# Expert stages of a two-block kernel: the steps of neighbouring expert pairs interleaved, with TensorE's order stated

## The chip, the cores and the metric

The kernel runs on one core of a Trainium2 chip. The metric is the device time of one execution in microseconds. The engines of a core run their own instruction queues in order: TensorE (PE; its weight loads are listed apart as PEld), VectorE (DVE), ScalarE (ACT), GpSimd (POOL) and SyncE (SP), which here issues the loads from HBM; they wait for each other through semaphores.

## The reference, cut to what matters

The program is two transformer blocks on 256 tokens of width 1024. The change concerns the hierarchical mixture of experts, which the second block computes twice, once in each of its two layers:

```python
def hier_moe(h, router_g, router_e, w1, w3, w2):
...
    pg = jax.nn.softmax(hf @ router_g.astype(f32), axis=-1)
    gi = jnp.argmax(pg, axis=-1).astype(jnp.int32)
...
    pk, ik = lax.top_k(jax.nn.softmax(le_sel, axis=-1), TOP_K)
    wts = pg_sel * pk / jnp.sum(pk, axis=-1, keepdims=True)
...
        return (jax.nn.silu(xi @ w1[e]) * (xi @ w3[e])) @ w2[e]
```

For each token a router picks one of four groups of eight experts and two experts in it; the two results are added with the router's weights. All 32 experts' w1, w3 (1024 x 512 each) and w2 (512 x 1024) are read in float32: six tiles of 1024 KB an expert, 192 a layer.

## The kernel before, in words

The function `moe` (line 1738) handles one layer. It gives each expert 64 places for tokens and takes the experts in 16 pairs; in a pair the two experts' tokens stand in the two halves of 128 columns, so that the matmuls of the two run side by side in TensorE's column halves (`tile_position`). The steps of a pair, in the generator `experts`, are:

- *gather* (line 1828): the tokens of four experts are selected by matmuls with 0/1 matrices, scaled (lines 1830 and 1831) and put into a buffer `xq`; half of a buffer with every pair, ahead of the two pairs that use it.
- *up* (line 1849): w1 and w3, two halves of the inner dimension, 32 matmuls of 64 columns by 512, into two PSUM banks `acc`.
- *pick* (lines 1856 to 1864): the selection matrix turned round, and the weights of the tokens.
- *hidden* (lines 1866 to 1868): tanh on ACT, two operations on VectorE, into a tile of the kind t2.
- *turn* (line 1872): four transposes into a bank `fb`, copied by ACT (line 1874) into another t2 tile.
- *down* (line 1884): w2, two halves c of the output, 16 matmuls into two `acc` banks.
- *evacuation* (lines 1888 to 1891): for each c a product with the gate on VectorE, a rounded copy on ACT and the remainder on VectorE, both t2 tiles.
- *scatter* (line 1895): for each c four matmuls that bring the result back to token order in a bank `mm`, added to x on VectorE (line 1896).

There are four `acc`, two `mm` and two `fb` banks, and four t2 tiles (two t2a, two t2b, taken in turn).

The weights of a stage are 192 tiles, loaded on SP's queue in the order of a list (`ExpertWeights`, line 1540, the load at line 1569) into a ring of 16 slots: nine shared with the large activations (`wa`), five (`w`) and two (`ww`). The first ones are loaded before the stage begins. `next` hands out the tiles in the order of the list, and issues the loads that follow in the ring.

Where each instruction stands in its engine's queue is not written out: a scheduler sets it when the program is built, from the program order as priority, the dependences and its own timing of them. After pair 28 (`OVER_AT`, line 180; pairs are named by their first expert) all loads that are left are issued and a test follows whether any expert has more than 64 tokens (`overflow`, line 1898); the branch behind it ends a block of the program, across which no instruction is moved. The last pair, 30, stands behind it.

Of the kernel before, what the change touches and what calls it, by code (L numbers as in the profile page):

```python
# [11 lines left out]
F32 = mybir.dt.float32  # L12
# [4 lines left out]
OP = mybir.AluOpType  # L17
# [190 lines left out]
def tile_blocks(ctx: ExitStack, tc: tile.TileContext, A, out):  # L208
# [1331 lines left out]
    class ExpertWeights:  # L1540
# [197 lines left out]
    def moe(l, x, cols_, router, weights):  # L1738
# [93 lines left out]

        gate = []

        def experts(xt, sel, ws_, load, n, s0=0, first=False):

            m = 64 * n
            ph = [bank("acc"), bank("acc")]  # L1840
            for kq in range(2):
                if first:
                    gather(sel, xt, kq)
                for i, nm in enumerate(("w1", "w3")):
                    w = [load(nm, e, kq) for e in range(n)]
                    for k in range(4):
                        for e in range(n):
                            sl = slice(64 * e, 64 * e + 64)
                            PE.matmul(ph[i][sl], xt[:, 4 * kq + k, s0 + 64 * e:s0 + 64 * e + 64],  # L1849
                                      w[e][:, k * 512:(k + 1) * 512], start=kq == 0 and k == 0, stop=kq == 1 and k == 3,  # L1850
                                      tile_position=(0, 64 * e))

            ps = bank("fb")
            f32 = [z.bitcast(F32) for z in sel]
            for t in range(2):
                PE.transpose(ps[:m, t * P:(t + 1) * P], f32[t][:, s0:s0 + m], ident)
            for e in range(n):
                for t in range(2):
                    PE.matmul(ps[64 * e:64 * e + 64, 256:257], f32[t][:, s0 + 64 * e:s0 + 64 * e + 64], ws_[:, t, e:e + 1],
                              start=t == 0, stop=t == 1, tile_position=(0, 64 * e), skip_group_check=True)  # L1860
            selw = temp(F32R)
            V.tensor_copy(selw[:m], ps[:m, :T])
            wsl_ = sm.tile([P, 1], F32, name="m_wsl", bufs=2)
            V.tensor_scalar(wsl_[:m], ps[:m, 256:257], 0.5, None, op0=OP.mult)
            th = temp2()
            S.activation(th[:m], ph[0][:m], AF.Tanh, scale=0.5)
            V.scalar_tensor_tensor(th[:m], th[:m], 1.0, ph[0][:m], op0=OP.add, op1=OP.mult)
            V.scalar_tensor_tensor(th[:m], th[:m], wsl_[:m], ph[1][:m], op0=OP.mult, op1=OP.mult)
            yield
            pt = bank("fb").rearrange("p (f s) -> p f s", s=P)  # L1870
            for f in range(4):
                PE.transpose(pt[:, f, :m], th[:m, f * P:(f + 1) * P], ident[:m, :m])
            ht = temp2().rearrange("p (f s) -> p f s", s=P)
            S.activation(ht[:, :, :m], pt[:, :, :m], AF.Copy)  # L1874
            if not gate:
                gate.append(gate_row(cols_, 5))
            gb, = gate
            py = [bank("acc"), bank("acc")]
            for c in range(2):
                w = [load("w2", e, c) for e in range(n)]  # L1880
                for f in range(4):
                    for e in range(n):
                        sl = slice(64 * e, 64 * e + 64)
                        PE.matmul(py[c][sl], ht[:, f, sl], w[e][:, f * 512:(f + 1) * 512], start=f == 0, stop=f == 3,  # L1884
                                  tile_position=(0, 64 * e))
            for c in range(2):
                cs = slice(c * 512, (c + 1) * 512)
                V.tensor_tensor(py[c][:m], py[c][:m], gb[:m, cs], op=OP.mult)  # L1888
                yh_, yl_ = temp2(F32R), temp2(F32R)
                S.activation(yh_[:m], py[c][:m], AF.Copy)  # L1890
                V.tensor_tensor(yl_[:m], py[c][:m], yh_[:m], op=OP.subtract)
                for t in range(2):
                    pa = bank(PAB)
                    for q in (yh_, yl_):
                        PE.matmul(pa, selw[:m, t * P:(t + 1) * P], q[:m], start=q is yh_, stop=q is yl_)  # L1895
                    V.tensor_tensor(x[:, t, cs], x[:, t, cs], pa, op=OP.add)  # L1896

        def overflow():

# [20 lines left out]
            with tc.If(many > 0):  # L1920
                V.scalar_tensor_tensor(slot, fq, -64.0, pos, op0=OP.mult, op1=OP.add)
                V.tensor_tensor(nx, xi, nx, op=OP.subtract)
                for t in range(2):
                    V.tensor_tensor(xid[:, t], fq[:, t], nx, op=OP.add)
                V.scalar_tensor_tensor(xid, fq, 0.0, xid, op0=OP.is_gt, op1=OP.mult)
                V.tensor_scalar(xid, xid, -1.0, None, op0=OP.add)
                V.memset(jt, 0.0)
                with tc.For_i(0, many, 1):
                    mk = st([2, 32], "mk")
                    V.tensor_scalar(mk, xid, jt, None, op0=OP.is_equal)  # L1930
                    sj = st([2, 32], "sj")
# [23 lines left out]
                    run(experts(xt, sel, sc[:, :, 1:2], load_at, 1, 0, True))  # L1955
# [93 lines left out]
```

## Time and profile before

| | |
|---|---|
| median of 3 runs | 2146.66 us (2145.38 to 2148.9) |
| the profiled execution | 2142.09 us, of which the span of its instructions is 2140.3 us |
| busy share of the span | PE 93%, PEld 59%, DVE 50%, ACT 29%, POOL 10% |
| HBM read | 585.95 MB, 276 GB/s over the span with what is written |
| weight tiles of the expert stages | 384 loads of 1024 KB (216 `wa`, 120 `w`, 48 `ww`) |
| up matmuls (line 1849) | 2048 records, about 600 ns each |

The two expert stages begin at 1022 and 1636 us, counted from the span's start. A busy time is the union of the records; TensorE's matmuls are pipelined and overlap, their ends are modelled, and each float32 matmul of 512 columns shows as two records. The idle time before an instruction is put down to the event that came last.

### The profile page before, as it was taken

The numbers are of one execution on the slowest core, as the hardware profiler recorded it, in microseconds if no ns is written. First come the engines' busy times: TensorE is split into PE (matmuls) and PEld (weight loads), VectorE is DVE, ScalarE is ACT, GpSimd is POOL, SyncE is SP. The second block draws the span as 40 slices with busy tenths as digits, with TensorE's granted clock in tenths as the row PEclk, the third lists the DMA queues.
The fourth block names the chain that finished last, engine by engine and source line by source line (L and its number), as shares of the span: only waits on it lengthen the run. The fifth ranks groups of instructions, "written<-read, shape, count | busy, mean of one in ns | idle before, by whom it ended". The sixth has DMA issues, their size and how long they took to land. (4 is left out here: it accounts for less than half of the span.)

```text
span 2140.3 us, 30475 instructions
## 1 busy us (share of the span) xinstructions
PE 1980.2 (93%) x12212; PEld 1256.9 (59%) x12212; DVE 1060.3 (50%) x2258; ACT 623.2 (29%) x1200; POOL 216.9 (10%) x419
## 2 busy tenths in 40 slices
PE   6999998999999899997999999998898999999896
PEld 5777787888988677776434333333795333333332
DVE  6787467866976477456323322222664233223223
ACT  4324655455555332433111111010442011111101
POOL 6475001110000160000000000000000000000000
PEclk8999999999999899999999999999998999999998
DMA  6532365545565236648799999997745999999992
GB/s 263 197 119 102 136 216 190 197 148 198 180 199 209 100 138 217 213 159 337 302 419 420 420 419 411 420 411 285 303 178 210 411 419 420 420 375 421 420 384 85
DMA packets 103650, 592.18 MB, mean 277 GB/s; under 512 B 30288, under 2 KB 30800, under 8 KB 32848
## 3 DMA queue, kind: packets, MB, share of 16 engines
q1 hardware_dynamic: 103360, 589.65, 70.3%
q8 instruction: 98, 1.61, 0.3%
q10 hardware_dynamic: 144, 0.52, 0.1%
q14 instruction: 48, 0.39, 0.1%
HBM read 585.95 MB, written 4.19 MB: 276 GB/s over the span
## 5 line engine op out<-in xcount | busy, mean ns | idle before, releaser
L1849 PE MATMUL acc<-wa,xq 128*64 128x512 f32 x1152 | 313.4, 602 | 2.5 <-DVEq L1920 2.5
L327 DVE TENSOR_TENSOR whl<-w,whl 128x1024 fp32r<-128x1024 f32 x203 | 255.2, 1258 | 111.7 <-ACT whl L325 109.9
L325 ACT ACTIVATE whl<-w 128x1024 fp32r<-128x1024 f32 x204 | 214.7, 1054 | 154.4 <-PE acc L405 71.0
L332 PE MATMUL mm<-hh,whl 128*128 128x256 f32 x736 | 215.1, 292 | 12.0 <-DVE hl L560 5.5
L334 PE MATMUL mm<-hh,whl 128*128 128x256 f32 x736 | 215.0, 292 | 2.0 <-DVE whl L327 1.9
L333 PE MATMUL mm<-hl,whl 128*128 128x256 f32 x736 | 212.3, 288 | 0.0
L1849 PEld LDWEIGHTS acc<-wa,xq 128*64 128x64 f32 x1152 | 93.1, 138 | 166.2 <-issue 157.5
L1849 PE MATMUL acc<-w,xq 128*64 128x512 f32 x640 | 183.0, 597 | 0.0
L332 PEld LDWEIGHTS mm<-hh,whl 128*128 128x128 f32 x736 | 145.2, 197 | 18.2 <-DVE hl L560 6.2
L334 PEld LDWEIGHTS mm<-hh,whl 128*128 128x128 f32 x736 | 144.9, 197 | 9.0 <-issue 4.0
L333 PEld LDWEIGHTS mm<-hl,whl 128*128 128x128 f32 x736 | 145.3, 197 | 1.3 <-issue 0.8
L1896 DVE TENSOR_TENSOR x<-x,mm 128x512 f32<-128x512 f32 x128 | 82.3, 684 | 93.9 <-PE mm L1895 93.9
L1888 DVE TENSOR_TENSOR acc<-acc,gb 128x512 f32<-128x512 f32 x64 | 44.8, 700 | 165.6 <-PE acc L1884 150.5
L1849 PEld LDWEIGHTS acc<-w,xq 128*64 128x64 f32 x640 | 54.3, 137 | 87.3 <-issue 83.5
L1830 DVE TENSOR_SCALAR xq<-mm,scnorm_ffn,ada_c 128x256 f32<-128x256 f32 x64 | 34.4, 543 | 128.2 <-PE mm L1828 67.5
L353 PE MATMUL mm<-hf,w 128*128 128x256 f32 x352 | 82.8, 384 | 1.9 <-DVE sz L1680 1.9
L1831 ACT ACTIVATE xq<-mm,ada_c,scnorm_ffn 128x256 f32<-128x256 f32 x64 | 35.6, 563 | 164.7 <-DVE xq L1830 164.7
L1884 PE MATMUL acc<-wa,t2b 128*64 128x512 f32 x288 | 74.5, 597 | 2.3 <-ACT t2b L1874 1.2
L1884 PE MATMUL acc<-wa,t2a 128*64 128x512 f32 x288 | 72.4, 596 | 2.3 <-ACT t2a L1874 1.2
L353 PEld LDWEIGHTS mm<-hf,w 128*128 128x128 f32 x352 | 64.5, 190 | 14.9 <-issue 2.4
L332 PE MATMUL acc<-hh,whl 128*128 128x256 f32 x224 | 66.0, 295 | 6.3 <-DVE x L583 5.6
L334 PE MATMUL acc<-hh,whl 128*128 128x256 f32 x224 | 65.2, 291 | 0.4 <-DVE whl L327 0.2
(812 smaller groups left out, 3765.5 us busy)
## 6 DMA issues: line engine op xcount, KB each, us to landing
wa<-in_w_dram SPq DMA_DIRECT2D x216, 1024.0 KB, 12.0
w<-in_w_dram SPq DMA_DIRECT2D x120, 1024.0 KB, 11.4
w<-in_ada_w_dram SPq DMA_DIRECT2D x48, 1024.0 KB, 4.9
ww<-in_w_dram SPq DMA_DIRECT2D x48, 1024.0 KB, 11.8
w<-in_w_up_dram SPq DMA_DIRECT2D x22, 1024.0 KB, 4.8
w<-in_wa_kv_dram SPq DMA_DIRECT2D x16, 1024.0 KB, 4.8
w<-in_wb_in_dram SPq DMA_DIRECT2D x12, 1024.0 KB, 4.8
w<-in_w_down_dram SPq DMA_DIRECT2D x11, 1024.0 KB, 4.8
```

The lines of the kernel that those rows point to most:

```text
L325: S.activation(h3, src, AF.Copy)
L327: (G if share and nsplit[0] % share == 0 else V).tensor_tensor(l3, src, h3, op=OP.subtract)
L332: PE.matmul(ps, ah, bh, start=start, stop=False)
L333: PE.matmul(ps, ah, bl, start=False, stop=False)
L334: PE.matmul(ps, al, bh, start=False, stop=stop)
L353: PE.matmul(ps, w3[:, k, j * P:(j + 1) * P], h[:, k], start=k == 0, stop=k == kt - 1)
L1830: V.tensor_scalar(xt[:, k0], ps[:, 0], a[:, k0:k0 + 1], b[:, k0:k0 + 1], op0=OP.mult, op1=OP.add)
L1831: S.activation(xt[:, k0 + 1], ps[:, 1], AF.Identity, scale=a[:, k0 + 1:k0 + 2], bias=b[:, k0 + 1:k0 + 2])
L1849: PE.matmul(ph[i][sl], xt[:, 4 * kq + k, s0 + 64 * e:s0 + 64 * e + 64], w[e][:, k * 512:(k + 1) * 512], start=kq == 0 and k == 0, stop=kq ...
L1884: PE.matmul(py[c][sl], ht[:, f, sl], w[e][:, f * 512:(f + 1) * 512], start=f == 0, stop=f == 3, tile_position=(0, 64 * e))
L1888: V.tensor_tensor(py[c][:m], py[c][:m], gb[:m, cs], op=OP.mult)
L1896: V.tensor_tensor(x[:, t, cs], x[:, t, cs], pa, op=OP.add)
```

## The change

The generator becomes a class with one method for each step, and the loop over pairs calls the steps of three pairs in turn: the turn of the pair before; the first half of up of this pair; the second scatter of the pair before last (`late`); the second half of up; pick and hidden; the gather; both halves of down of the pair before; its first scatter. `tc.issue_after(ins)` gives every instruction in its block that runs on the engine of `ins` (here TensorE) an edge of order behind `ins`, without a wait for its end. Before the overflow test and at the end of the stage a pair is finished by `rest`, without a neighbour. The list of loads is put in the same order: the w2 tiles of a pair behind the w1 and w3 tiles of the next.

```diff
@@ class ExpertWeights: the order of the loads @@
-            self.todo = [(nm, (l * 32 + e + j) * 2 + i) for e in range(0, 32, 2)
-                         for i, nm in ((0, "w1"), (0, "w3"), (1, "w1"), (1, "w3"), (0, "w2"), (1, "w2"))
-                         for j in range(2)]
+            ups, downs = ((0, "w1"), (0, "w3"), (1, "w1"), (1, "w3")), ((0, "w2"), (1, "w2"))
+            order, before = [], None
+            for e in range(0, 32, 2):
+                order += [(e, w) for w in ups] + [(before, w) for w in downs if before is not None]
+                before = e
+                if e == OVER_AT:
+                    order += [(e, w) for w in downs]
+                    before = None
+            order += [(before, w) for w in downs]
+            self.todo = [(nm, (l * 32 + e + j) * 2 + i) for e, (i, nm) in order for j in range(2)]
...
@@ the steps: a generator becomes a class with a method for each step @@
-        def experts(xt, sel, ws_, load, n, s0=0, first=False):
+        class Experts:
...
+            def up(self, kq):
...
+                return nc.cur_bb.bb.instructions[-1]
...
+            def turned(self):
...
+            def down(self, c):
...
+                py = bank("acc")
+                w = [self.load("w2", e, c) for e in range(self.n)]
...
+                last = nc.cur_bb.bb.instructions[-1]
+                V.tensor_tensor(py[:m], py[:m], gb[:m, c * 512:(c + 1) * 512], op=OP.mult)
                 yh_, yl_ = temp2(F32R), temp2(F32R)
-                S.activation(yh_[:m], py[c][:m], AF.Copy)
-                V.tensor_tensor(yl_[:m], py[c][:m], yh_[:m], op=OP.subtract)
+                S.activation(yh_[:m], py[:m], AF.Copy)
+                V.tensor_tensor(yl_[:m], py[:m], yh_[:m], op=OP.subtract)
+                self.y[c] = yh_, yl_
+                return last
...
+            def scatter(self, c):
...
+            def rest(self, late=None):
+
+                if late:
+                    late.scatter(1)
+                self.turned()
+                self.down(0)
+                with tc.issue_after(self.down(1)):
+                    for c in range(2):
+                        self.scatter(c)
...
@@ the loop over pairs in moe @@
+        before = late = None
         for e in range(0, 32, 2):
-            now = experts(xt, sel, wtf[:, :, e:e + 2], load, 2, 64 * (e % 4), e == 0)
-            next(now)
-            if e % 4 == 0 and e < 28:
-                nxt, nsel = big("xq", (8, 256)), slots(pos[:, :, e + 4:e + 8], 4)
-            if e < 28:
-                gather(nsel, nxt, e % 4 // 2)
-            run(now)
-            if e % 4 == 2:
+            now = Experts(xt, sel, wtf[:, :, e:e + 2], load, 2, 64 * (e % 4))
+            if before:
+                with tc.issue_after(behind):
+                    before.turned()
+            if e == 0:
+                gather(sel, xt, 0)
+            behind = now.up(0)
+            if late:
+                with tc.issue_after(behind):
+                    late.scatter(1)
+            if e == 0:
+                gather(sel, xt, 1)
+            behind = now.up(1)
+            now.picked()
+            now.hidden()
+            with tc.issue_after(behind):
+                if e % 4 == 0 and e < 28:
+                    nxt, nsel = big("xq", (8, 256)), slots(pos[:, :, e + 4:e + 8], 4)
+                if e < 28:
+                    gather(nsel, nxt, e % 4 // 2)
+                if before:
+                    before.down(0)
+                    behind = before.down(1)
+            if before:
+                with tc.issue_after(behind):
+                    before.scatter(0)
+            before, late = now, before
+            if e % 4 == 2 and e < 28:
                 xt, sel = nxt, nsel
             if e == OVER_AT:
+                before.rest(late)
+                before = late = None
                 weights.fill(192)
                 overflow()
+        before.rest(late)
```


The arithmetic of the steps stays. What stands outside the two expert stages keeps its order on every engine.

TensorE's queue in the program before, in the first layer, from the end of the up matmuls of one pair (lines 1849 up, 1872 turn, 1856 and 1859 pick, 1884 down):

```order
L1849 MATMUL acc<-wa,xq 64x512 x24
L1872 MATMUL fb<-ident,t2b 128x128 x4
L1856 MATMUL fb<-ident,t1b 128x128
L1856 MATMUL fb<-ident,t1a 128x128
L1859 MATMUL fb<-m_wt,t1b 64x1
L1859 MATMUL fb<-m_wt,t1a 64x1
L1859 MATMUL fb<-m_wt,t1b 64x1
L1859 MATMUL fb<-m_wt,t1a 64x1
L1884 MATMUL acc<-wa,t2a 64x512
```

The turn stands right behind up, and down right behind the turn and the pick.

TensorE's queue in the program before, the same pair, from the end of the first half of down to its scatter matmuls (line 1895; 1849 is the next pair's up):

```order
L1884 MATMUL acc<-wa,t2a 64x512
L1884 MATMUL acc<-w,t2a 64x512 x2
L1895 MATMUL mm<-t2b,t1a 128x512 x2
L1895 MATMUL mm<-t2a,t1a 128x512 x2
L1884 MATMUL acc<-w,t2a 64x512 x7
L1895 MATMUL mm<-t2b,t1a 128x512 x2
L1895 MATMUL mm<-t2a,t1a 128x512 x2
L1849 MATMUL acc<-w,xq 64x512
```

The first scatter stands one matmul behind the first half of down, the second right behind the second half. The first splits a couple of down matmuls, as the count of 7 behind it shows.

TensorE's queue in the changed program, in the first layer, from the gather (1835) over both halves of down (1903) and the first scatter (1919) to the turn (1889):

```order
L1835 MATMUL mm<-t1a,xh 128x256
L1835 MATMUL mm<-t1a,xl 128x256
L1903 MATMUL acc<-w,t2a 64x512 x8
L1903 MATMUL acc<-ww,t2a 64x512 x8
L1919 MATMUL mm<-t2a,t1b 128x512
L1919 MATMUL mm<-t2b,t1b 128x512
L1919 MATMUL mm<-t2a,t1b 128x512
L1919 MATMUL mm<-t2b,t1b 128x512
L1889 MATMUL fb<-ident,t2b 128x128 x4
```

Both halves of down now stand behind a gather, the first scatter behind both of them, and the turn, which is the next pair's, behind that.

TensorE's queue in the changed program, going on from that turn (1867 and 1870 pick, 1858 up, 1919 the second scatter):

```order
L1889 MATMUL fb<-ident,t2b 128x128 x4
L1867 MATMUL fb<-ident,t1b 128x128
L1867 MATMUL fb<-ident,t1a 128x128
L1870 MATMUL fb<-m_wt,t1b 64x1
L1870 MATMUL fb<-m_wt,t1a 64x1
L1870 MATMUL fb<-m_wt,t1b 64x1
L1870 MATMUL fb<-m_wt,t1a 64x1
L1858 MATMUL acc<-wa,xq 64x512 x16
L1919 MATMUL mm<-t2a,t1b 128x512
L1919 MATMUL mm<-t2b,t1b 128x512
L1919 MATMUL mm<-t2a,t1b 128x512
L1919 MATMUL mm<-t2b,t1b 128x512
```

Behind the turn and a pick come 16 up matmuls, and only then the second scatter of the pair whose down stood above.

## Rows read from the trace of the kernel before

**Rows 1.** Windows, both stages (busy us by engine, PEclk, DMA, GB/s).

```profile
1022.00:1472.00 450.00, 427.18 (x2012) 167.30 (x2010) 129.58 (x230) 53.48 (x94) 0.00 (x0) 1.00 0.99 408
...
1473.00:1485.00 12.00, 11.25 (x58) 4.28 (x60) 1.08 (x3) 0.00 (x0) 0.00 (x0) 1.00 0.01 3
...
1636.00:2094.00 458.00, 430.69 (x2012) 167.80 (x2010) 129.22 (x230) 53.45 (x93) 0.00 (x0) 0.99 0.98 401
...
2094.00:2125.00 31.00, 27.55 (x118) 9.33 (x117) 6.37 (x11) 3.13 (x7) 0.00 (x0) 0.94 0.01 3
```

**Rows 2.** The page: GB/s of the DMA in 40 slices.

```profile
GB/s 263 197 119 102 136 216 190 197 148 198 180 199 209 100 138 217 213 159 337 302 419 420 420 419 411 420 411 285 303 178 210 411 419 420 420 375 421 420 384 85
```

**Rows 3.** Source view of line 1872 (ns min/median/max, first, last start).

```profile
L1872 PE MATMUL fb<-ident,t2b x64: 272/273/331, 1041.6 to 1490.6; 128*128 128x128 f32 x64
...
L1872 PE MATMUL fb<-ident,t2a x64: 272/273/330, 1655.7 to 2114.0; 128*128 128x128 f32 x64
```

**Rows 4.** Timeline: first up of each stage, VectorE behind the last w2.

```profile
1021.98 0.64 PE L1849 MATMUL acc<-wa,xq 128*64 128x512 f32 x2
...
1501.72 0.70 DVE L1888 TENSOR_TENSOR acc<-acc,gb 128x512 f32<-128x512 f32 x1 [2.53 <-PE acc L1884]
...
1636.03 0.64 PE L1849 MATMUL acc<-wa,xq 128*64 128x512 f32 x2
...
2125.16 0.70 DVE L1888 TENSOR_TENSOR acc<-acc,gb 128x512 f32<-128x512 f32 x1 [2.53 <-PE acc L1884]
```

**Rows 5.** Waits of TensorE, 14 pairs of each stage (us, times, longest).

```profile
PE fb L1872 <- DVE t2b L1868: 9.2, 11, 0.9
...
PE mm L1895 <- ACT t2b L1890: 8.6, 8, 1.4
...
PE mm L1895 <- ACT t2a L1890: 12.5, 12, 1.4
...
PE fb L1872 <- DVE t2a L1868: 9.2, 11, 0.9
```

**Rows 6.** Timeline of TensorE: a pair with waits (idle in brackets).

```profile
1399.90 0.66 PE L1872 MATMUL fb<-ident,t2b 128*128 128x128 f32 x4 [0.88 <-DVE t2b L1868]
...
1406.41 0.73 PE L1895 MATMUL mm<-t2b,t1a 128*128 128x512 f32 x2 [0.67 <-ACT t2b L1890]
...
1412.87 0.73 PE L1895 MATMUL mm<-t2b,t1a 128*128 128x512 f32 x2 [1.42 <-ACT t2b L1890]
```

**Rows 7.** Timeline of TensorE: a pair nearly without waits.

```profile
1099.84 0.60 PE L1872 MATMUL fb<-ident,t2b 128*128 128x128 f32 x4
...
1101.12 7.09 PE L1884 MATMUL acc<-wa,t2a 128*64 128x512 f32 x32
...
1112.23 1.07 PE L1849 MATMUL acc<-wa,xq 128*64 128x512 f32 x2
...
1113.23 0.73 PE L1895 MATMUL mm<-t2a,t1a 128*128 128x512 f32 x2
...
1128.47 0.60 PE L1872 MATMUL fb<-ident,t2b 128*128 128x128 f32 x4
```

**Rows 8.** Source view of line 1569: loads from 1028, then from 1642.

```profile
L1569 SPq DMA_DIRECT2D wa<-in_w_dram x98: 327/328/1363, 1028.4 to 1441.1; - x98
...
L1569 SPq DMA_DIRECT2D w<-in_w_dram x55: 327/328/1034, 1047.9 to 1454.7; - x55
...
L1569 SPq DMA_DIRECT2D ww<-in_w_dram x22: 327/328/384, 1060.2 to 1458.1; - x22
...
DMA to landing us min/median/max: 4.8/12.7/18.0
...
L1569 SPq DMA_DIRECT2D wa<-in_w_dram x98: 327/328/423, 1642.6 to 2062.9; - x98
```

**Rows 9.** Windows, two stretches of the second stage (columns as Rows 1).

```profile
1875.00:1900.00 25.00, 23.12 (x108) 9.25 (x110) 5.33 (x11) 2.73 (x5) 0.00 (x0) 0.93 1.01 415
...
2025.00:2050.00 25.00, 22.91 (x94) 9.00 (x93) 6.44 (x10) 2.47 (x5) 0.00 (x0) 0.93 0.85 343
```

More of the change, by code (lines that the diff above doesn't have):

```diff
@@ L1833, in moe, with __init__ @@
         gate = []
-        def experts(xt, sel, ws_, load, n, s0=0, first=False):
[L1839 to L1843, printed above, removed]
+        class Experts:
+            def __init__(self, xt, sel, ws_, load, n, s0=0):
+                self.xt, self.sel, self.ws_, self.load, self.n, self.s0, self.m = xt, sel, ws_, load, n, s0, 64 * n
+                self.ph = [bank("acc"), bank("acc")]
+                self.y = [None, None]
+            def up(self, kq):
@@ L1844, in experts @@
                 for i, nm in enumerate(("w1", "w3")):
-                    w = [load(nm, e, kq) for e in range(n)]
+                    w = [self.load(nm, e, kq) for e in range(self.n)]
                     for k in range(4):
[L1847 to L1857, printed above, removed]
-                for t in range(2):
-                    PE.matmul(ps[64 * e:64 * e + 64, 256:257], f32[t][:, s0 + 64 * e:s0 + 64 * e + 64], ws_[:, t, e:e + 1],
-                              start=t == 0, stop=t == 1, tile_position=(0, 64 * e), skip_group_check=True)
-            selw = temp(F32R)
@@ L1862, in experts @@
[L1862 to L1880, printed above, removed]
-                for f in range(4):
-                    for e in range(n):
+                        for e in range(self.n):
+                            sl, c = slice(64 * e, 64 * e + 64), self.s0 + 64 * e
+                            PE.matmul(self.ph[i][sl], self.xt[:, 4 * kq + k, c:c + 64], w[e][:, k * 512:(k + 1) * 512],
+                                      start=kq == 0 and k == 0, stop=kq == 1 and k == 3, tile_position=(0, 64 * e))
@@ new lines, in up, with picked @@
+                return nc.cur_bb.bb.instructions[-1]
+            def picked(self):
+                ps, m, s0 = bank("fb"), self.m, self.s0
+                f32 = [z.bitcast(F32) for z in self.sel]
+                for t in range(2):
+                    PE.transpose(ps[:m, t * P:(t + 1) * P], f32[t][:, s0:s0 + m], ident)
+                for e in range(self.n):
+                    for t in range(2):
+                        PE.matmul(ps[64 * e:64 * e + 64, 256:257], f32[t][:, s0 + 64 * e:s0 + 64 * e + 64],
+                                  self.ws_[:, t, e:e + 1], start=t == 0, stop=t == 1, tile_position=(0, 64 * e),
+                                  skip_group_check=True)
+                self.selw = temp(F32R)
+                V.tensor_copy(self.selw[:m], ps[:m, :T])
+                self.wsl = sm.tile([P, 1], F32, name="m_wsl", bufs=2)
+                V.tensor_scalar(self.wsl[:m], ps[:m, 256:257], 0.5, None, op0=OP.mult)
@@ new lines, in hidden @@
+            def hidden(self):
+                m, ph = self.m, self.ph
+                th = self.th = temp2()
+                S.activation(th[:m], ph[0][:m], AF.Tanh, scale=0.5)
+                V.scalar_tensor_tensor(th[:m], th[:m], 1.0, ph[0][:m], op0=OP.add, op1=OP.mult)
+                V.scalar_tensor_tensor(th[:m], th[:m], self.wsl[:m], ph[1][:m], op0=OP.mult, op1=OP.mult)
+            def turned(self):
+                m = self.m
+                pt = bank("fb").rearrange("p (f s) -> p f s", s=P)
+                for f in range(4):
+                    PE.transpose(pt[:, f, :m], self.th[:m, f * P:(f + 1) * P], ident[:m, :m])
+                self.ht = temp2().rearrange("p (f s) -> p f s", s=P)
+                S.activation(self.ht[:, :, :m], pt[:, :, :m], AF.Copy)
@@ L1883, in experts @@
+            def down(self, c):
+                if not gate:
+                    gate.append(gate_row(cols_, 5))
+                gb, m = gate[0], self.m
+                py = bank("acc")
+                w = [self.load("w2", e, c) for e in range(self.n)]
+                for f in range(4):
+                    for e in range(self.n):
                         sl = slice(64 * e, 64 * e + 64)
-                        PE.matmul(py[c][sl], ht[:, f, sl], w[e][:, f * 512:(f + 1) * 512], start=f == 0, stop=f == 3,
+                        PE.matmul(py[sl], self.ht[:, f, sl], w[e][:, f * 512:(f + 1) * 512], start=f == 0, stop=f == 3,
@@ L1885, in experts @@
                                   tile_position=(0, 64 * e))
-            for c in range(2):
-                cs = slice(c * 512, (c + 1) * 512)
-                V.tensor_tensor(py[c][:m], py[c][:m], gb[:m, cs], op=OP.mult)
+                last = nc.cur_bb.bb.instructions[-1]
+                V.tensor_tensor(py[:m], py[:m], gb[:m, c * 512:(c + 1) * 512], op=OP.mult)
                 yh_, yl_ = temp2(F32R), temp2(F32R)
-                S.activation(yh_[:m], py[c][:m], AF.Copy)
-                V.tensor_tensor(yl_[:m], py[c][:m], yh_[:m], op=OP.subtract)
+                S.activation(yh_[:m], py[:m], AF.Copy)
@@ L1892, in experts @@
+                V.tensor_tensor(yl_[:m], py[:m], yh_[:m], op=OP.subtract)
+                self.y[c] = yh_, yl_
+                return last
+            def scatter(self, c):
+                m, cs = self.m, slice(c * 512, (c + 1) * 512)
                 for t in range(2):
                     pa = bank(PAB)
-                    for q in (yh_, yl_):
-                        PE.matmul(pa, selw[:m, t * P:(t + 1) * P], q[:m], start=q is yh_, stop=q is yl_)
+                    for i, q in enumerate(self.y[c]):
+                        PE.matmul(pa, self.selw[:m, t * P:(t + 1) * P], q[:m], start=i == 0, stop=i == 1)
@@ L1953, in load_at @@
                         return over
-                    run(experts(xt, sel, sc[:, :, 1:2], load_at, 1, 0, True))
+                    one_ = Experts(xt, sel, sc[:, :, 1:2], load_at, 1)
+                    for kq in range(2):
+                        gather(sel, xt, kq)
+                        one_.up(kq)
+                    one_.picked()
+                    one_.hidden()
+                    one_.rest()
                     V.tensor_scalar(jt, jt, 1.0, None, op0=OP.add)
```

## The prediction

> **What bounds the kernel now.** I read the windows of the two expert stages first, then what TensorE waits for in them, then single pairs in its timeline, then the weight loads, and last the ends of both stages.
>
> The reader is to see that two things are full at once. While the stage runs, the DMA engines are busy 0.99 and 0.98 of the time and TensorE 0.95 and 0.94 [rows 1]. One pair of experts is 12 tiles of 1 MB; at the 420 GB/s of the full slices a tile takes 1.0486 / 0.420 = 2.50 us [rows 2], a pair 30.0 us. TensorE's period is (1490.6 − 1041.6) / 15 = 29.9 us in the first stage and (2114.0 − 1655.7) / 15 = 30.6 in the second [rows 3]. The loads run in a ring of 16 slots, and a slot is given back by TensorE, so either side can hold the other.
>
> Which one ends last is decided at the ends. From 1473 to 1485 and from 2094 to 2125 the DMA share is 0.01 while TensorE works on [rows 1]; the last w2 matmul is done at 1501.7 and 2125.2, where VectorE takes it over [rows 4]. So about 30 us of landed weights lie unused when the stream ends. TensorE is the later of the two, and what it waits for is worth time until that stock is gone.
>
> It never waits for a load in the stretch of 14 pairs. It waits for ACT before the scatter matmuls (8.6 and 12.5 us) and for VectorE before the turning transposes (9.2 and 9.2) [rows 5]. In one bad pair this is 0.88 before the transposes, 0.67 before the first scatter and 1.42 before the second [rows 6]: each time the next step of the same pair stands next in TensorE's queue while its input is still being evacuated. (The gap shown is less than the loss, since the ends of the matmuls before it are modelled.)
>
> **The change part by part.**
>
> *Order of TensorE's steps.* Nothing is added or taken away: 32 up, 16 down, 8 scatter, 16 gather and 4 turn matmuls in a pair, and six small ones (an up or down matmul shows as two records). Moved: the turn goes behind the down matmuls of the pair before; down goes one pair later, behind the next pair's up and gather; the first scatter stands behind both halves of down; the second stands behind 8 to 16 up matmuls. What each used to wait for now runs beside 7 us of down, 3.5 us of the other half of down, or 3.4 us or more of up. The chain that these must cover is an evacuation of some 2 us, so I cost the waits at nothing; if the cover is gone (last pair before the overflow test, and the last pair of a stage, where nothing is interleaved) they stay as they are today.
>
> *Lone matmuls.* Two experts' matmuls run side by side in the two column halves: 32 records take 7.09 us. Where a scatter splits such a couple, 2 records alone take 1113.23 − 1112.23 = 1.00 us [rows 7]. The pair from 1099.84 to 1128.47 has no wait over 0.2 us and takes 28.6 us [rows 7], with four lone matmuls, that is two steps of 0.86 us lost. In the new order most pairs have none. 28.6 − 1.7 + 0.2 for one more change of kind = **27.1 us a pair**, against 30.0 of the loads.
>
> *TensorE's bound then.* Today a stage is 1501.7 − 1022.0 = 479.7 us = 16 × 29.9 + 1.3. New: 16 × 27.1 + 1.3, and about 8 us for the uncovered chains of the last two pairs: 443 us, ending at 1465 and, from 1636.0, at 2079 [rows 4].
>
> *Loads.* The list gives w2 one pair later, so it stays the order in which TensorE frees and needs the tiles; the same 192 tiles, each released by the last matmul that reads its slot. SP's queue holds the loads alone in this stretch, so nothing else is held up. 98 + 55 + 22 = 175 loads are issued after the ring is first full, from 1028.4; the quickest takes 4.8 us to land, 2.3 more than its transfer [rows 8]. 1028.4 + 2.3 + 175 × 2.5 = 1468.2. Today it is 1472, so some 4 us are lost to late slots; I keep 2 of them: 1470. The last two tiles land together and 16 of the 32 down records follow, 3.5 us: **1473.5**. This is later than TensorE's 1465: the loads bound the stage, with a margin of 8.5 us or 0.5 us a pair. In the second stage the loads begin at 1642.6 [rows 8]: 1642.6 + 2.3 + 437.5 + 2 + 3.5 = **2087.9**.
>
> *New waits.* Four tiles of the kind t2 carry six values a pair, and the hidden activations now keep theirs until the turn. So VectorE's subtraction for the second half must wait for the turn; behind it in VectorE's queue stand the selection copy and the adds that free the scatter banks. The turn is the next thing after the first scatter, and the second scatter comes 8 or more up matmuls later, so I take 0. No row shows this wait; its bounds are 0 and the 1.42 us of today's longest [rows 6], below nothing not, since it takes no work away. The same for the four acc banks: two for up, two for down, each evacuated one step before its next use: 0.
>
> *Clock.* TensorE will now wait for loads in the last third of a stage. Waiting has cost clock here: two stretches of 25 us have a granted clock of 0.93 [rows 9], that is 3.5 us at 1.2 GHz instead of 2.4, or 1.75 us of work each. Most of that is hidden by the slack of 2.9 us a pair; I charge one such drop behind the last landing of each stage, 3.5 us in all; bounds 0 and 16 (below).
>
> *Sum.* (1501.7 − 1473.5) + (2125.2 − 2087.9) − 3.5 = 28.2 + 37.3 − 3.5 = 62.0 us. All between the stages and behind them keeps its order and shifts. The profiled execution took 2142.1 us, so it would take 2080; the median of the three runs is 4.6 us higher, so in its terms **2085 us**.
>
> **The rivals.**
>
> *Waits remain.* If a pair keeps 1.2 us of waits (today's mean pair is 29.9 − 28.6 = 1.3 above the clean one), TensorE ends 16 × 1.2 − 8.5 = 10.7 us later in each stage than the loads allow: 2085 + 21 = 2106. For: the scheduler chose some rows (early pairs still split couples). Against: in the steady rows every step has its cover. Chance 0.12.
>
> *The clock falls in the waits for loads.* The loads are 2.9 us a pair slower than TensorE, so it stops at every two tiles. If each stop cost a drop of 1.75 us, six a pair would be 10.5 us; but a TensorE behind the loads doesn't wait, so the period stays near 30 and only the end counts: the last pair's 28 us, partly before the last landing. At half clock I put 8 us a stage behind it: 2085 − 3.5 + 16 = 2097. For: the two drops [rows 9]; against: they are two in 29 pairs with 2 to 3 us of waits. Chance 0.14. The Trainium skill ("TensorE: Matmul & The Clock Gate", section "HAM oscillation — how this bites in real kernels") speaks for this rival: where a tile's matmuls are shorter than the wait for the next tile's data, the clock falls in every such wait and each tile begins slow. By that rule the time is this rival's 2097; the matmuls of two tiles (3.5 us) are here longer than the wait I expect (1.5 us), and no run here shows waits of that kind yet.
>
> *No change.* The DMA engines are the full resource, and an order that only moves TensorE's waits from evacuations to landings ends at the same time, 2147. For: shares of 0.99 and 0.98. Against: 30 us of work behind the last landing, which a shorter period must eat. Chance 0.03. The Trainium skill ("Perfetto Trace Analysis", section "Identifying the Most-Contended Engine") would have the engine with the highest share improved first, which here is the DMA; by it the sum would be this 2147. The trace agrees on the share, not on who ends last.
>
> *Slower: the t2 tiles.* If VectorE stands at the subtraction until the turn, and the turn in its turn waits for a bank that an add behind that subtraction must free, both evacuations of a pair lie open: three times today's 1.42 a pair, 4.3 us. Then 27.1 + 4.3 = 31.4, and the stages end at 1022.0 + 16 × 31.4 + 9.3 = 1533.7 and 2147.7: 32 and 22.5 us later than today, 2201. It decides from waits of 3 us a pair, where the period passes 30. For: four tiles for six values. Against: the order puts the turn ahead of the second scatter. Chance 0.05.
>
> **How the numbers follow.** Forecast 0.66, the four rivals 0.34. Within 0.2% (4.3 us, about what a measurement of this kernel can tell from no change): 0.03; slower 0.05; faster 0.92. The range: low end with no clock cost (−3.5), none of the 4 us lost in the loads (−4) and runs that lie as low as the profile did (−4.6): 2073, taken as 2072; high end a little above the waits rival, 2110. That leaves out no change, slower and the tails of the others, less than 2 in 10.
>
> **What would show it.** Right: TensorE's waits for ACT before scatter and for VectorE before the turn nearly gone; a period of about 27 us in the first ten pairs (28 us of stock, 2.9 a pair) and 30 in the last ones, there with waits for loads; the last w2 matmul 3 to 5 us behind the last landing, not 30; DMA share without holes. Wrong: a period above 28.5 with waits for ACT or VectorE (first rival); a clock of 0.8 or less in the last 100 us of a stage (second); last landings later than 1473 and, 28 us shifted, 2059 (the stream slowed by the new order); VectorE's subtraction waiting for TensorE in every pair (the last).

## The result and the profile after

The changed kernel takes 2087.9 us in the median (2087.6 to 2091.4, 4 runs) against 2146.0 (2143.9 to 2148.9): a ratio of 0.9732, with an interval of 0.9715 to 0.9749. The forecast was 2085, the range 2072 to 2110. The profiled execution has a span of 2085.8 us, where the one before had 2140.3. In the table of the experiments one run of the kernel with the test behind the last pair, 2233.5 us at a granted clock of 0.835, is left out of its median.

First the windows of the two expert stages of the kernel after, which answer to [rows 1], then the GB/s of its page, which answer to [rows 2].

```profile
1025.14:1472.00 446.86, 436.01 (x2096) 183.24 (x2095) 131.25 (x236) 55.45 (x95) 0.00 (x0) 1.00 0.99 411
1472.00:1479.00 7.00, 7.00 (x32) 2.71 (x28) 1.39 (x2) 1.08 (x2) 0.00 (x0) 1.00 0.99 410
1615.40:2064.00 448.60, 439.07 (x2094) 183.87 (x2094) 131.43 (x236) 55.33 (x95) 0.00 (x0) 1.00 0.99 410
2064.00:2071.00 7.00, 7.00 (x34) 2.41 (x31) 1.72 (x3) 0.60 (x1) 0.00 (x0) 1.00 0.01 6
```

```profile
GB/s 270 202 101 122 133 192 194 182 192 162 201 198 182 124 143 186 233 182 203 277 420 419 419 419 419 420 419 419 379 217 167 356 419 419 420 419 419 419 420 265
```

When the last tile of a stage lands is read from the source view of the loads, cut to the last of them: its issue plus its time to landing. After, both stages:

```profile
L1576 SPq DMA_DIRECT2D ww<-in_w_dram x1: 327/327/327, 1454.1 to 1454.1; - x1
...
DMA to landing us min/median/max: 21.3/21.3/21.3
...
L1576 SPq DMA_DIRECT2D ww<-in_w_dram x1: 328/328/328, 2044.9 to 2044.9; - x1
...
DMA to landing us min/median/max: 21.2/21.2/21.2
```

Before, where the last load of the first stage is issued at 1458.1 [rows 8]:

```profile
DMA to landing us min/median/max: 16.3/16.3/16.3
...
L1569 SPq DMA_DIRECT2D ww<-in_w_dram x1: 328/328/328, 2080.0 to 2080.0; - x1
...
DMA to landing us min/median/max: 15.9/15.9/15.9
```

So the last tile now lands at 1475.4 and 2066.2 (2044.91 + 21.25 before rounding); before it was 1474.4 and 2095.9. The 0.01 behind 2064 in the last of the windows says that nearly all bytes are through by then, not that the last tile counts as landed. (In the first stage loads for the next part of the program follow at once, so the share stays at 0.99 behind 1472.) In no whole slice between the first load and the last does the rate fall under 419 GB/s any more; before there were slices of 411 and 375.

The two ends of the stages in the timeline answer to [rows 4]: the first up matmul, and VectorE taking over the last w2 matmul.

```profile
1025.14 2.34 PE L1858 MATMUL acc<-wa,xq 128*64 128x512 f32 x9
...
1479.16 0.70 DVE L1906 TENSOR_TENSOR acc<-acc,gb 128x512 f32<-128x512 f32 x1 [1.99 <-PE acc L1903]
...
1615.41 1.06 PE L1858 MATMUL acc<-wa,xq 128*64 128x512 f32 x4
...
2070.67 0.70 DVE L1906 TENSOR_TENSOR acc<-acc,gb 128x512 f32<-128x512 f32 x1 [1.38 <-PE acc L1903]
```

TensorE's last w2 matmul thus follows the last landing by 3.7 and 4.5 us, where it was 27.3 and 29.3 before. The stages take 454.0 and 455.3 us instead of 479.7 and 489.1 [rows 4]: 25.7 + 33.8 = 59.5 us. The span fell by 54.5. The other 5 us are outside the change: this execution came to the first stage 3.2 us later (1025.14 against 1021.98) and took 136.3 us between the stages instead of 134.3; in a repetition of the same kernel the first up matmul stood at 1027.9.

The waits of TensorE over 14 pairs of the first stage, in the view of [rows 5], all of them:

```profile
PE acc L1858 <- DMA w<-in_w_dram: 2.1, 2, 1.3
PE acc L1858 <- DMA ww<-in_w_dram: 1.6, 2, 0.9
PE acc L1858 <- DMA wa<-in_w_dram: 1.5, 2, 0.8
```

Nothing is left there of the waits before the scatters and before the turn; what TensorE waits for now is weights. (In the last two pairs, which have no neighbour, they remain. The rows of the weight loads, PEld, show more than those of the matmuls, whose ends are modelled: 15.1 us of waits for weights in the same stretch, in 14 places.) The timeline of one early pair, in the view of [rows 6, 7], shows why, with the steps one behind the other and no bracket:

```profile
1236.10 0.60 PE L1889 MATMUL fb<-ident,t2b 128*128 128x128 f32 x4
...
1244.11 0.50 PE L1919 MATMUL mm<-t2a,t1a 128*128 128x512 f32 x1
...
1254.36 7.09 PE L1903 MATMUL acc<-wa,t2a 128*64 128x512 f32 x32
1261.37 0.51 PE L1919 MATMUL mm<-t2a,t1b 128*128 128x512 f32 x1
...
1262.42 0.60 PE L1889 MATMUL fb<-ident,t2b 128*128 128x128 f32 x4
```

From turn to turn it is 26.3 us, with whole couples of matmuls and the second scatter (at 1244.1) in the middle of the next pair's up. The period has two parts, read from the turns in TensorE's timeline:

```profile
1071.56 0.66 PE L1889 MATMUL fb<-ident,t2b 128*128 128x128 f32 x4
...
1289.72 0.66 PE L1889 MATMUL fb<-ident,t2b 128*128 128x128 f32 x4
...
1409.43 0.66 PE L1889 MATMUL fb<-ident,t2b 128*128 128x128 f32 x4
```

Seven pairs from 1071.56 to 1262.42 take 27.3 us each, without a wait; the four from 1289.72 to 1409.43 take 29.9, the pace of the loads. The windows of the second stretch:

```profile
1289.70:1409.40 119.70, 115.26 (x538) 48.59 (x536) 33.61 (x59) 14.06 (x24) 0.00 (x0) 1.00 1.01 420
```

### The profile page after: what moved, and what is told of

The parts are those of the page before. It is cut to its first block, busy times and chain, and to the rows that moved or that the text cites. A ratio compares the mean times of both kernels' runs of the same rounds, so it can differ in the third digit from the quotient of the medians.

```text
span 2085.8 us, 30511 instructions
## 1 busy us (share of the span) xinstructions
PE 1961.0 (94%) x12212; PEld 1277.7 (61%) x12212; DVE 1057.8 (51%) x2258; ACT 624.6 (30%) x1200; POOL 217.1 (10%) x419
## 5 line engine op out<-in xcount | busy, mean ns | idle before, releaser
L1858 PE MATMUL acc<-wa,xq 128*64 128x512 f32 x1168 | 304.7, 600 | 5.6 <-DMA wa<-in_w_dram 3.1
L1858 PEld LDWEIGHTS acc<-wa,xq 128*64 128x64 f32 x1168 | 101.0, 137 | 168.3 <-issue 148.0
L1858 PE MATMUL acc<-w,xq 128*64 128x512 f32 x656 | 188.7, 597 | 4.0 <-DMA w<-in_w_dram 4.0
L1858 PEld LDWEIGHTS acc<-w,xq 128*64 128x64 f32 x656 | 63.6, 137 | 74.4 <-issue 59.9
L333 PE MATMUL acc<-hl,whl 128*128 128x256 f32 x224 | 64.5, 288 | 0.0
## 6 DMA issues: line engine op xcount, KB each, us to landing
wa<-in_w_dram SPq DMA_DIRECT2D x216, 1024.0 KB, 19.9
w<-in_w_dram SPq DMA_DIRECT2D x120, 1024.0 KB, 19.9
ww<-in_w_dram SPq DMA_DIRECT2D x48, 1024.0 KB, 19.9
```

The lines of the kernel that those rows point to most:

```text
L333: PE.matmul(ps, ah, bl, start=False, stop=False)
L1858: PE.matmul(self.ph[i][sl], self.xt[:, 4 * kq + k, c:c + 64], w[e][:, k * 512:(k + 1) * 512], start=kq == 0 and k == 0, stop=kq == 1 and k ...
```

## Experiments

The theory: TensorE's period needs only to fall below what the loads allow; from there on the loads set the end, and no further wait of TensorE counts. The rivals: TensorE is the bound throughout, so every wait is worth its length; or the list of loads, or the tracing in the interleaved order, does it alone. The length of a stage, from the first up matmul to the end of the last w2 matmul, is the best measure, since what lies outside differs by some us between executions; it is read from one profiled execution each. The ratios are to the kernel before, run beside each:

| kernel | median us | ratio to before, 95% | stage 1 | stage 2 |
|---|---|---|---|---|
| before | 2146.0 | | 479.7 | 489.1 |
| after | 2087.9 | 0.9715 to 0.9749 | 454.0 | 455.3 |
| after, repeated | 2089.4 | 0.9708 to 0.9752 | 454.8 | 455.1 |
| late scatters alone | 2098.2 | 0.9732 to 0.9807 | 458.2 | 460.0 |
| scatters at once | 2091.2 | 0.9718 to 0.9760 | 455.6 | 458.9 |
| no stated order | 2152.6 | 1.0009 to 1.0051 | 489.1 | 486.1 |
| old list of loads | 2158.7 | 1.0034 to 1.0074 | 488.5 | 492.5 |
| more gather | 2091.5 | 0.9723 to 0.9777 | 455.4 | 457.0 |
| test behind the last pair | 2093.8 | 0.9724 to 0.9769 | 455.0 | 454.8 |

### Late scatters alone

The list of loads of before, turn and down inside their own pair, and only the scatters moved and their place stated:

```diff
+            behind = now.up(0)
+            if before:
+                with tc.issue_after(behind):
+                    before.scatter(0)
...
+            behind = now.up(1)
+            if before:
+                with tc.issue_after(behind):
+                    before.scatter(1)
             now.picked()
             now.hidden()
+            with tc.issue_after(behind):
...
+                now.turned()
+                now.down(0)
+                now.down(1)
```

> Only the scatters are late here: the list of loads and the order up, turn, down inside a pair are those of the kernel before, and each scatter is stated to stand behind half of the next pair's up. Theory (TensorE needs only to fall below what the loads allow, 28.2 us a pair averaged from the second pair to the fourteenth of the changed kernel): the wait before the turn stays, about 0.9 us a pair, the waits before the scatters and most lone matmuls go, TensorE's own pair is about 28.0 us, and the end is the loads' end again: 2083 to 2095. Rival (every wait of TensorE is worth its length to the end): the turn's wait and the one before down, 1.0 us in 32 pairs, come on top of the changed kernel: about 2120.

Measured: 2098.2 us (2089.7 to 2104.4, 4 runs), 3 above the theory's range and 22 under the rival. The period is even shorter than in the changed kernel: from the turn at 1073.87 to that at 1206.10 five pairs take 26.4 us each. The expectation had the wait before the turn wrong: up to 1445 us nothing over 0.2 us is left of it here either. TensorE's timeline at the end of one pair:

```profile
1201.51 3.60 PE L1851 MATMUL acc<-ww,xq 128*64 128x512 f32 x16
1205.05 0.50 PE L1912 MATMUL mm<-t2b,t1b 128*128 128x512 f32 x1
...
1206.10 0.60 PE L1882 MATMUL fb<-ident,t2b 128*128 128x128 f32 x4
```

The second scatter now stands between up and turn and covers VectorE's last operation on the hidden activations with its 1.05 us, where in the bad pairs of before the turn came directly behind up. And still the stages are 4 to 5 us longer. From the seventh pair on TensorE stands at the loads; its waits, and the windows of that stretch:

```profile
PE acc L1851 <- DMA w<-in_w_dram: 5.3, 5, 1.4
PE acc L1851 <- DMA wa<-in_w_dram: 3.9, 5, 0.8
PE acc L1851 <- DMA ww<-in_w_dram: 3.1, 4, 1.0
```

```profile
1206.00:1445.00 239.00, 226.31 (x1073) 100.36 (x1072) 68.13 (x119) 28.13 (x48) 0.00 (x0) 1.00 1.01 420
```

With 1.01 for the DMA share and 420 GB/s there is nothing to win from a faster TensorE in that stretch. Most of what the stages lack comes at their end: the last w2 matmul stands 6.7 and 8.4 us behind the last landing instead of 3.7 and 4.5. So most of the gain can be had without interleaving up and down of neighbouring pairs: with stated places for the scatters alone the two stages lack 9 us of it, 50.6 instead of 59.5.

### Scatters at once

The changed kernel, but both scatters directly behind their own down, and the next steps stated behind them:

```diff
-            behind = now.up(0)
+            with tc.issue_after(behind) if before else ExitStack():
+                behind_ = now.up(0)
+            behind = behind_
...
                 with tc.issue_after(behind):
                     before.scatter(0)
-            before, late = now, before
+                    before.scatter(1)
+                behind = nc.cur_bb.bb.instructions[-2]
+            before, late = now, None
```

> The interleaving and the list of loads stay, but both scatters of a pair stand directly behind its down, and the next steps are stated behind them, so that the second scatter waits for its evacuation in every pair, 1.4 us or a little more. Theory (the loads take what TensorE can't use): TensorE's own pair is 27.3 + 1.4 = 28.7 us, 0.5 over what the loads allow, so some 8 us a stage: about 2104, between 2096 and 2112. Rival (every wait is worth its length): 1.4 us in 32 pairs: about 2133.

Measured: 2091.2, 5 below the theory's range and 42 under the rival. The waits are there in nearly every pair, but at most 0.6 us long instead of 1.4 (the view covers 12 pairs of the first stage):

```profile
PE mm L1919 <- DVE x L1920: 3.8, 6, 0.6
PE mm L1919 <- ACT t2a L1908: 2.4, 6, 0.4
```

The pairs from 1076.94 to 1415.81 take 28.2 us each, 12 of them, and no matmul waits for a load there: the stock of loaded tiles lasts. The stages are 1.6 and 3.6 us longer than in the changed kernel, not 8. Three orders with TensorE's own pair at 26.4, 27.3 and 28.2 us thus end within 9 us of one another, where each 0.9 us a pair in 32 pairs would be 29 us. Late scatters, then, are not needed either where up and down are interleaved: what the three kernels share is that the order is stated, and the next experiment takes just that away.

### No stated order

The steps are traced in the interleaved order, and the loads come in the new list, but every `issue_after` is taken away:

```diff
-                with tc.issue_after(behind):
+                with ExitStack():
                     late.scatter(1)
...
```

> All steps are traced in the interleaved order and the list of loads is the new one, but no order is stated, the scheduler may choose. The built order has 130 runs of up or down matmuls of an odd number, each with a lone matmul at its end, against 34 in the changed kernel and 102 before; at 0.43 us each that is 41 us over both stages, 1.3 us a pair. Theory: TensorE's own pair is 28.6 us and more where a wait is left bare, above what the loads allow: 2105 to 2135, about 2118. Rival (the interleaved tracing is enough, the stated order does nothing): 2088, and no wait before a scatter or the turn.

Measured: 2152.6, above the range of the theory and 0.1 to 0.5% slower than before; the rival (the tracing is enough) is out. The lone matmuls were counted in the expectation, the waits were not. TensorE's timeline of one pair:

```profile
1211.75 0.59 PE L1903 MATMUL acc<-w,t2a 128*64 128x512 f32 x1
1213.83 0.73 PE L1919 MATMUL mm<-t2a,t1b 128*128 128x512 f32 x2 [1.48 <-ACT t2a L1908]
...
1215.21 3.22 PE L1903 MATMUL acc<-ww,t2a 128*64 128x512 f32 x13
...
1220.34 0.73 PE L1919 MATMUL mm<-t2a,t1b 128*128 128x512 f32 x2 [1.48 <-ACT t2a L1908]
```

The scheduler puts each scatter in as soon as it thinks its input ready, in the middle of down and of the next up. TensorE then stands 1.48 us at both, and each time a couple is split. Over 13 pairs of the first stage there are 15 such waits, 22.2 us in all. The interleaved order has the cover for these waits; without the statement the scheduler uses it up.

### Old list of loads

The changed kernel's order, but w2 of a pair loaded ahead of the next pair's w1 and w3, as before. A load is still issued only within 16 tiles of the oldest tile that is not yet handed out:

```diff
-            for e in range(0, 32, 2):
-                order += [(e, w) for w in ups] + [(before, w) for w in downs if before is not None]
...
+            self.todo = [(nm, (l * 32 + e + j) * 2 + i) for e in range(0, 32, 2)
+                         for i, nm in ((0, "w1"), (0, "w3"), (1, "w1"), (1, "w3"), (0, "w2"), (1, "w2"))
+                         for j in range(2)]
...
+                self.fill(next(m for m in range(193) if m not in self.used) + SLOTS)
```

> TensorE's order is stated as in the changed kernel, but the weights are loaded in the order of the list before: w2 of a pair ahead of the next pair's w1 and w3, though it is read behind them. Theory: four tiles of w2 hold the ring, no load beyond the sixteenth tile from them can be issued until down has read them, and TensorE then waits for w1 and w3 in every pair: eight tiles behind down are 18.8 us, then 3.5 of up, 8 of turn and down, 2 of gather: about 32 us a pair and 2200; at the least 2140. The DMA share then falls under 0.97, with holes. Rival (the list only decides which transfer goes first): 2088.

Measured: 2158.7, inside the theory's bounds though below its middle; from the turn at 1068.4 to the one at 1435.1 twelve pairs take 30.6 us, not 32, and the DMA share while the loads run (1031 to 1476 and 1655 to 2098 us) is 1.00 and 0.99, not under 0.97, so that part of the expectation failed. The holes are there, but short. The worst pair in TensorE's timeline, and its window:

```profile
1284.73 1.32 PE L1852 MATMUL acc<-w,xq 128*64 128x512 f32 x2 [3.35 <-DMA w<-in_w_dram]
1287.23 1.12 PE L1852 MATMUL acc<-w,xq 128*64 128x512 f32 x2 [1.19 <-DMA w<-in_w_dram]
```

```profile
1284.00:1310.00 26.00, 24.08 (x96) 8.80 (x98) 3.95 (x7) 1.16 (x2) 0.00 (x0) 0.87 0.88 361
```

While w2 keeps four slots of the ring, w1 and w3 come late, and then the stream itself pauses. TensorE's matmuls wait 21.6 us for weights between 1068 and 1466 us, and the granted clock is 0.98 and 0.97 over the two stages, by estimate 0.02 × 488.5 + 0.03 × 492.5 = 25 us of work. So the last w2 matmul comes 31.7 and 32.9 us behind the last landing: TensorE is the later one again. How the 71.7 us of the two stages split is not settled: the built order of this kernel also has 90 odd runs of up or down matmuls against 34, at 0.43 us by estimate some 24 us at the most, since the scheduler chose other rows.

### More gather

The changed kernel with half as many gather matmuls again:

```diff
-                for k in (k0, k0 + 1):
+                for k in (k0, k0, k0 + 1):
```

> The changed kernel with TensorE's gather half as long again: one of each two products is computed twice into the same bank, 8 matmuls or 0.95 us in 14 of 16 pairs, 13 us a stage. Theory (the loads set the end from the middle of a stage on): TensorE's own pair goes from 27.3 to 28.2 us, its waits for loads, some 10 us in pairs 10 to 13 of the first stage, go away, and only what is left comes out: 3 to 5 us a stage, about 2096, between 2088 and 2104. Rival (TensorE is the bound): all 27 us come out, 2115.

Measured: 2091.5, inside the theory's range; in the stages 1.4 and 1.8 us come out of 13.3 each, less than the 3 to 5 that it named. Twelve pairs from 1070.16 to 1408.68 take 28.2 us, as expected, and the waits of TensorE up to the last pair hold no load at all:

```profile
PE acc L1858 <- DVEq L1954: 1.2, 1, 1.2
PE fb L1889 <- DVE t2b L1883: 1.0, 1, 1.0
...
PE acc L1903 <- ACT t2a L1891: 0.7, 1, 0.7
```

The 12 us of added work took the place of the waits for loads, 15.1 us in the rows of the weight loads above. That is TensorE's slack in a stage of the changed kernel, and the rival (TensorE is the bound, 2115) is out.

### The test behind the last pair

`OVER_AT` at 30, so that the last two pairs are interleaved as well:

```diff
-    OVER_AT = 28
+    OVER_AT = 30
...
```

> The changed kernel with the test for overflowing experts behind the last pair and not behind the one before it, so that the last two pairs are interleaved too. Theory: in the first stage the last w2 matmul ends 7.4 us behind the last landing, in the second 5, of which 3.5 are the last tiles' own matmuls; these 4 and 1.5 us go, and the branch, 1.25 us and a drain, comes at the end of each stage instead: within 4 us of the changed kernel, 2084 to 2092. Rival (the uncovered chains of the last two pairs cost the 8 us a stage that the prediction gave them): 2075.

> The changed kernel itself, on the same chip as the two others: 2085 to 2092, as before.

Measured: 2093.8, 2 above the theory's range, beside 2089.4 for the changed kernel on the same chip; the intervals overlap. The stages take 455.0 and 454.8 us, against 454.8 and 455.1 without it. The 8 us of uncovered chains a stage that the rival wanted back don't come. The expectation's 7.4 us behind the last landing in the first stage were misread: by the landings above it is 3.7. No kernel here beats the changed one.

## Why the prediction was right

**What bounds.** "TensorE is the later of the two, and what it waits for is worth time until that stock is gone": right. The stock of before, the time from the last landing to the last w2 matmul, was 27.3 and 29.3 us; 3.7 and 4.5 are left, and then the loads took over. In the second stage about 10 of the 33.8 us come from the stream itself, which the forecast had too: from the first load behind the start to the last landing it took 2095.9 − 1642.6 = 453.3 us and now takes 443.2. The added gather shows the other side of it, 12 us of work for 1.5.

**TensorE's period.** Forecast 27.1, measured 27.3. Its two parts were sized a little differently: the lone matmuls did not all go. The built order has 34 runs with an odd number of matmuls instead of 102. By estimate, at 0.43 us each, that is 29 us in 32 pairs, 0.9 us a pair and not the 1.5 net that the sum took; the waits would then have given the more, 29.9 − 27.3 − 0.9 = 1.7 us. No run separates the two. Where no couple is split the pair takes 26.3.

**Loads, the term that was mis-sized.** The rows of the loads in the two stages:

```profile
L1576 SPq DMA_DIRECT2D wa<-in_w_dram x98: 327/328/1244, 1032.2 to 1436.7; - x98
...
DMA to landing us min/median/max: 4.8/19.9/21.5
...
L1576 SPq DMA_DIRECT2D wa<-in_w_dram x98: 327/328/423, 1623.0 to 2027.5; - x98
```

From the first of the 175 loads to the last landing the forecast gave 441.6 and 441.8 us; measured are 1475.4 − 1032.2 = 443.2 and 2066.2 − 1623.0 = 443.2. The step that failed is "today it is 1472, so some 4 us are lost to late slots; I keep 2 of them". The 1472 was the edge of a window; the last tile landed at 1474.4, so 6.2 us were lost before, and 443.2 − 2.3 − 437.5 = 3.4 are lost now. Besides, the first load was issued 7.1 and 7.6 us behind the first up matmul instead of 6.4 and 6.6.

The median from issue to landing has gone from 12.7 [rows 8] to 19.9: loads now stand in the queue, since slots come free sooner than the engines can fill them.

**The tail.** The step "the last two tiles land together and 16 of the 32 down records follow, 3.5 us" nearly held: 3.7 and 4.5 us, inside the 3 to 5 us that the prediction named as a sign of being right. With the 1.6 and 1.4 of the loads and the 0.7 and 1.0 of the first load, the stages come out 2.5 and 3.4 us longer than the forecast's 451.5 and 451.9. (The last landings stand 450.3 and 450.7 us behind the first up matmul, where the sign of a slowed stream was 451 and more.) But the margin of 8.5 us between TensorE's 1465 and the loads' 1473.5 was not there. TensorE stood at loads until 1434, and its uncovered chains of the last two pairs came only then, when no slack was left. The end of the first stage, TensorE's matmuls and one of its weight loads:

```profile
1434.13 3.65 PE L1903 MATMUL acc<-ww,t2a 128*64 128x512 f32 x14 [1.25 <-DMA ww<-in_w_dram]
...
1454.06 3.65 PE L1858 MATMUL acc<-wa,xq 128*64 128x512 f32 x16 [1.25 <-DVEq L1954]
...
1470.08 0.63 PE L1889 MATMUL fb<-ident,t2b 128*128 128x128 f32 x4 [0.93 <-DVE t2b L1883]
1471.40 3.65 PE L1903 MATMUL acc<-w,t2a 128*64 128x512 f32 x16 [0.69 <-ACT t2a L1891]
1474.88 4.25 PE L1903 MATMUL acc<-ww,t2a 128*64 128x512 f32 x16
...
1475.48 0.83 PEld L1903 LDWEIGHTS acc<-ww,t2a 128*64 128x64 f32 x6 [0.46 <-DMA ww<-in_w_dram]
```

TensorE waits for the overflow test (1454), VectorE and ACT, and still comes to the last tile 0.46 us before it has landed. In the second stage it comes 0.9 us late (2067.0 against 2066.2). So these chains cost a stage less than 1 us, which agrees with the experiment before this section: putting the overflow test behind the last pair changed the stages by 0.4 us at the most, beside the repeated run. That the two came out level was luck; the sum had TensorE well ahead.

**Clock.** 3.5 us were charged for two drops behind the last landings. The granted clock is 1.00 in both windows behind 1472 and 2064 above. One drop shows in the second stage, behind the overflow test; TensorE's windows there:

```profile
2044.87:2050.15 5.28, 5.28 (x16) 1.74 (x16) 0.00 (x0) 0.00 (x0) 0.00 (x0) 0.68 1.01 410
```

At 0.68 of the clock over 5.28 us it costs by estimate 0.32 × 5.28 = 1.7 us of work, of which no more than the 0.9 us that TensorE comes late to the last tile can have reached the stage's end. So this charge was too high by 2.6 us at least, and that paid for a part of what the loads and the tail took more.

**Sum.** The stages gave 59.5 where 62.0 was forecast, and 5 us were lost outside: 2087.6 against 2080 for the profiled execution. In the median the difference is only 2.9, by luck: the sum added 4.6 us for runs longer than the profiled one, and after the median lies 0.3 above it.

**The rivals.** *Waits remain*: none in 14 pairs of the first stage. *The clock falls in the waits for loads*: no, in two kernels. In the changed one TensorE stands at loads between 1289.7 and 1409.4, and in the kernel with the late scatters 12.3 us in all, no wait longer than 1.4: the granted clock is 1.00 in both. The old list shows the other case: with waits of 3.35 and 1.19 us in one pair it is 0.87 over 26 us. The Trainium skill ("TensorE: Matmul & The Clock Gate", section "HAM oscillation — how this bites in real kernels") tells of a kernel in which each tile's matmuls are shorter than the wait for the next tile's data and the clock falls in every such wait. The traces agree as far as they go: the matmuls' waits of up to 1.4 us, shorter than the 3.5 us of two tiles' matmuls, left the clock alone, and the one of 3.35 us, about as long as them, came with a fall; no run here shows a fall in every wait. The prediction's reason for setting this rival at 0.14 held. *No change*: the engine with the highest share was not the one to relieve first. *The t2 tiles*: in the source view of VectorE's subtraction (line 1909, first stage) it waits for ACT's copy alone, never for TensorE:

```profile
L1909 DVE TENSOR_TENSOR t2b<-acc,t2a x28: 680/691/694, 1072.3 to 1439.7; 128x512 fp32r<-128x512 f32 x28
...
  ACT t2a L1908: 13.7, 19
```

## What to carry to other kernels

Where two resources are both near full, look at what lies behind the end of the one and ask who is late there; a wait of the other is worth time only up to that stock, and past it a still shorter period bought nothing here (26.4 us a pair with the late scatters alone against 27.3). An order that leaves cover for each wait has to be stated to the scheduler, which otherwise spends the cover: the same steps without the statement gave back all 58 us. When reading order changes, the list that fills a ring has to change with it. The end of a stream is the landing of its last load, issue and time to landing added, not the edge of a window; 2 to 3 us hung on that here. And chains without cover are to be counted at the very end, after the slack has gone, not against a margin over the whole stage.

## What was not expected of the hardware

In the kernel with the late scatters alone the loads run at a share of 1.01 and 420 GB/s, and TensorE's matmuls stop for 0.5 to 1.4 us ten times and more in 240 us without its clock leaving 1.00. And with the loads as the bound, the largest hole left is at the start of a stage, where the ring is full and TensorE has not yet freed a slot. The windows of the changed kernel:

```profile
1017.00:1033.00 16.00, 13.14 (x68) 7.83 (x70) 6.72 (x33) 1.33 (x3) 0.00 (x0) 0.76 0.00 2
```

That is 16 us at a DMA share of 0.00; the first load behind it is issued at 1032.2. No kernel here tried to fill it.
